# A hybrid attention and delta-rule layer on one core: TensorE's order in the attention stage from fixed to ranked, and its loads moved

## The chip, the core and the metric

The kernel runs on one core of a Trainium2 chip. A core has five engines with queues of their own: TensorE (PE, matrix products, with weight loads shown as PEld), VectorE (DVE), ScalarE (ACT), GpSimd (POOL) and SyncE (SP, which here only issues DMAs). They wait for each other by semaphores. The metric is the device time of one execution in microseconds; smaller is better. Times below are the median of three runs, and the profile is that of one more execution.

## The reference

One layer of a streaming encoder, 1024 frames of 1024 features, float32:

```
u = RMSNorm(h)
p = u @ W_in            # attention q, k, v | delta q, k, v | gate | decay | beta
A = attention(q, k, v)  # 8 heads of 64; each chunk of 64 frames sees itself and 8 chunks before;
                        # q and k normalised per head; bias by clipped distance; softmax
B = gated delta rule    # 4 heads of 128: short causal convolution + SiLU, L2-normalised q, k,
                        # S <- S * decay + k^T (v - k S), output q S, gated RMSNorm per head
h = h + concat[RMSNorm(A), B] @ W_out
h = h + relu(RMSNorm(h) @ W1)^2 @ W2        # 4096 hidden features
```

The output is the (1, 1024, 1024) result.

## The kernel before, in words

A float32 product is made of three products of split operands (`split`: a rounded high part by ScalarE, the low part by VectorE or GpSimd), so a product of large matrices is three matmuls for each step (`mm3`).

The program has four stages. First the input projections for delta k, q, v, the gate, attention k and q and most of attention v, with the preparation of the recurrence beside them. Then the stage that the change touches, `attention`, in which attention, the recurrence, the last two value projections and the beginning of the output projection share TensorE. Then the rest of the output projection, and then the feed-forward layer, `ffn`, whose two halves `ff1` and `ff2` use Strassen-like products of blocks (`product`, q1 to q7 and p1 to p7).

Attention works in 32 units: two groups `g` of four heads, eight tiles `t` of 128 frames, two pairs of heads `pp`. For a unit `score` makes the scores against the newest keys (`t_sb`) and the older ones (`t_sa`), VectorE adds the bias and finds the row limit (L936, L947), ScalarE takes the exponential (L955, L959); `flip` transposes the result on TensorE (`t_tpb`, `t_tpa`) and copies it out by whichever of the two engines is free (`t_tb`, `t_ta`); `multiply` makes the product with the values for both units of a tile (`t_o`), `finish` turns and scales it (`t_on`), `turn` transposes the normalised tile for the output projection (`t_tpo`, `mixa`). The recurrence (`delta_all`) has eight chunks of 128 frames with the steps M (`delta_merge`, `m_tp`, `m_p`), S (`delta_state`, `c_tpv`, `c_pk`, `c_pv`, `c_pq`, `c_pS`), O (`delta_out`, `c_Ltd`, `c_tpq`, `c_mt`, `c_po`) and F (`delta_fin`, `c_tpo`, `mixd`).

All of these share eight PSUM banks: three for scores and projections (`ps_a`), two for transpositions of attention (`ps_t`), one for its output (`ps_o`), two for the recurrence (`ps_d`). Pages of SBUF come from pools by tag; a tile gets a page when an earlier one with the tag is released. Queries of a tile take a page of the tag "x", of which there are two (`start`, L884); biases, keys and values take pages of "u", "dk", "wl" and others as the projections release them.

The order of work is written by a planner: the loop from L1083 keeps a simulated clock (`Clock`) with costs for TensorE, the other engines and the banks, and at each point issues the step that can run soonest, with ties by a rank. START (5000 ns) holds back the first score. The block around it,

```
    with tc.manual_schedule(engines={mybir.EngineType.PE}):
        rest = attention(after[NV - 1], delta_all(ab, kT, W), values, lambda: out_proj(result))
```

keeps TensorE's instructions in exactly the order in which the planner wrote them. On every other engine, and on TensorE outside this block, the scheduler of the language decides at compile time: it goes through the program with its own model of time and issues on each engine, among the instructions whose operands it holds ready, the one that stands first in the code (`tc.high_priority()` moves one ahead; `tc.issue_after(x)` keeps one behind x on its engine). The order that comes out is fixed in the program; on the chip each engine follows its own queue and waits where an operand is late.

The loads of the stage are issued by SyncE. Biases and values first get a small copy on GpSimd from the sixth value projection's result (`after`), so that they don't load earlier. `load_rest` (L869) names the older biases, the remaining values and keys, before tile (0, 2) is scored; the biases of the second group follow at tile (0, 6).

In `ff2`, for each of four blocks of the hidden features, the seven products have operands that VectorE prepares (`prep5`, `prep3`, `prep6`, `prep7`, `prep4`) and that are then split. `early` is the last split of the second product (p5); the first subtraction of `prep3` and of `prep7` is kept behind it on VectorE.

Of the kernel before, what the change touches and what calls it, by code (L numbers as in the profile page):

```python
# [11 lines left out]
ALU = mybir.AluOpType  # L12
# [6 lines left out]
NT = SEQ // P  # L19
# [21 lines left out]
DELTA = 71e3  # L41
LATENCY, MARGIN = 250, 400
LEAD = 0.1
START = 5000
NV = 6


# [52 lines left out]
def hymba_kernel(  # L100
# [20 lines left out]
    nc = tc.nc  # L121
# [708 lines left out]
    def attention(after, delta, values, outputs):  # L830
# [16 lines left out]
        def load_old(g):  # L847
            for i in range(4):
                b = bias_page("u", f"biaso{g}{i}")
                nc.sync.dma_start(out=b[:, 0:384], in_=bias_win[4 * g + i, :, 0:384])  # L850
                nc.gpsimd.memset(b[64:128, 0:64], NEG)
                old[g].append(b)
# [13 lines left out]
                nc.sync.dma_start(out=tl, in_=v_dr[t])  # L866
                vt.append(tl)

        def load_rest():  # L869
            load_old(0)  # L870
            load_values((2, 3))
            load_keys(0, 1)
            load_values(range(4, NT))
            load_keys(1, 0)
            load_keys(1, 1)

        keys, old, new, vt = [[[], []], [[], []]], [[], []], [[], []], []
        load_keys(0, 0)
        load_new(0)
        load_values((0, 1))  # L880

        tiles, outs = {}, {}

        def start(g, t):  # L884
            n = f"t{g}{t}"
            T = dict(n=n, k0=max(0, t - 4))
            T["kb"] = max(0, t - 1)
            if (g, t) == (1, 1):
                T["q"] = [page("on", f"{n}_q{m}", F32R) for m in range(2)]
                for r0 in (0, 64):  # L890
                    for m in range(2):
                        nc.sync.dma_start(out=T["q"][m].bitcast(F32)[r0:r0 + 64], in_=q_dr[t, :, m, g, :])
            else:
                q = page("x", n + "_q", F32R, w=DM)
                qf = q.bitcast(F32)
                for r0 in (0, 64):
                    nc.sync.dma_start(out=qf[r0:r0 + 64].rearrange("p (m c) -> p m c", m=2), in_=q_dr[t, :, :, g, :])
                T["q"] = [part(q, m) for m in range(2)]
            T["sums"] = small("t", n + "_sum", 8)
            T["nm"] = small("t", n + "_nm", 8)  # L900
            T["s"], T["p"], T["done"] = {}, {}, {}
            tiles[g, t] = T

        def product(g, T, i, bk, off, ka, kb):
# [157 lines left out]
        total, spent, deltas, begun, multiplied = sum(size), 0, 0, 0, 0  # L1062
        ready, later, live = [], [], {}
        banks = clock.banks
        groups = delta
        fed = next(groups)

# [15 lines left out]
        while True:  # L1083
# [20 lines left out]
                todo.append((at(flipping[1]), 3, "flip"))  # L1104
            if begun < len(units) and begun - multiplied < 5 and (begun - flipped < 3):
                a = banks["a"]
                todo.append((max(a[0], a[1] - 500, a[2] - 900, START if not begun else 0), 4, "score"))
            if values_left:
                todo.append((banks["a"][0], 7, "values"))
            elif flipped == len(units) and not live.keys() - {"F"} and not any(p[1] is finish and p[2][1] < NT - 1 for p in later):  # L1110
# [10 lines left out]
            if k in live:  # L1121
                gen = live[k][0]
                before = clock.now
                want = next(gen, None)
                deltas += clock.now - before
                if want is None:
                    del live[k]
                else:
                    live[k] = gen, want
            elif k == "multiply":  # L1130
                for n in units[multiplied:multiplied + 2]:
                    multiply(*n)
                    pe(218 * size[multiplied])
                pe(300)
                spent += 2 * size[multiplied]
                t = give("o", on("s", 366, clock.now + LATENCY, ahead=True))
                later.append((t, finish, units[multiplied][0:2]))
                multiplied += 2
            elif k == "later":
                _, step, args = later.pop(0)  # L1140
                step(*args)
                if step is finish:
                    t = give("t", on("v", 420, pe(220), ahead=True))
                    if args[0]:
                        t = on("v", 853, on("g", 3200, on("s", 780, t)))
                        later.append((t + MARGIN, turn, args[1:]))
                        later.sort(key=lambda p: p[0])
                else:
                    give("t", on("v", 682, pe(440), ahead=True))
            elif k == "flip":  # L1150
                want = next(flipping[0], None)
                flipping = want and (flipping[0], want)
                if want is None:
                    flipped += 1
            elif k == "score":
                g, t, pp = units[begun]
                if pp == 0:
                    start(g, t)
                    if (g, t) == (0, 2):
                        load_rest()  # L1160
                    if (g, t) == (0, 6):
                        load_new(1)
                        load_old(1)
                score(g, t, pp)
                begun += 1
            elif k == "values":
                if next(values, None) is None:
                    values_left = False
                else:
                    give("a", on("s", 690, pe(5500)))  # L1170
            else:
                next(outputs_gen)
                pe(690)
                fill += 1
# [231 lines left out]
    def ff2(psw, pools):  # L1406
# [7 lines left out]

        y = {i: [wide(t, 0), wide(t, 1)] for i, t in y.items()}
        y[7] = [page2("y7", f"y7_{i}") for i in range(2)]
        side, splits = [0], []

        def load_h(t, j, hf, m):
            nc.sync.dma_start(out=two(t), in_=h_dr[j, hf, :, 2 * m:2 * m + 2, :])  # L1420
# [1 line left out]
        def product(name, prep, by_rows=False):  # L1422
# [11 lines left out]
            for i in range(2):  # L1434
                ab = []
                for o, src in zip("ab", prep(i)):
                    hi = page2("h" + t, f"{name}{o}{i}_h", F32R)
                    lo = page2("l" + t, f"{name}{o}{i}_l", F32R)
                    splits.append(split(src, hi, lo, nc.scalar, nc.vector)[1])
                    ab.append((hi, lo))  # L1440
                ops.append(ab)
                if not by_rows:
                    for k in range(2):
                        for q in range(4):
                            step(i, k, q)
# [13 lines left out]
        for kb in range(nb):  # L1459
# [50 lines left out]
                return s1[i], b11[i]  # L1510

            def prep3(i):
                with tc.issue_after(early):
                    tt(s1[i], s1[i], a11[i], ALU.subtract)
                tt(a12[i], a12[i], s1[i], ALU.subtract)
                return a12[i], b22[i]

# [2 lines left out]
                return s1[i], b11[i]  # L1520

            def prep7(i):
                with tc.issue_after(early):
                    tt(a21[i], a11[i], a21[i], ALU.subtract)
                tt(b12[i], b22[i], b12[i], ALU.subtract)
                return a21[i], b12[i]

# [3 lines left out]

            accumulate(1, product(f"p1{kb}", lambda i: (a11[i], b11[i])))
            accumulate(5, product(f"p5{kb}", prep5))
            early = splits[-1]
            accumulate(2, product(f"p2{kb}", lambda i: (a12[i], b21[i])))
            if last:
                merge(nc.gpsimd, 2, 1)
# [49 lines left out]
    kT = []  # L1587
# [16 lines left out]
                 att_proj(u, AK, "k"), att_proj(u, AQ, "q"), first_steps(values, NV)), 1.0),  # L1604
        (chained(delta_prep(kT, ab), (1000 for _ in delta_low(0, W, "pp"))), 0.35))
    clock.reset()
    with tc.manual_schedule(engines={mybir.EngineType.PE}):
        rest = attention(after[NV - 1], delta_all(ab, kT, W), values, lambda: out_proj(result))
    for _ in rest or ():
        pass  # L1610
    mixer.close()
# [50 lines left out]
```

## Time and profile before

| what | value |
|---|---|
| median of 3 runs | 1301.49 us (1301.42 to 1302.32) |
| the profiled execution, its time | 1301.99 us |
| its span, first to last instruction | 1300.1 us |
| TensorE busy | 96% of the span |
| VectorE, ScalarE, GpSimd busy | 72%, 42%, 22% |
| mean granted TensorE clock | 0.984 |
| bytes moved by DMA | 158.53 MB, 122 GB/s in the mean |

In the rows of the profile a line such as "371.69 1.19 PE L916 MATMUL t_sb<-ks,t_q ... x4 [6.97 <-DMA t_q<-q_dr]" reads: from 371.69 us for 1.19 us, TensorE, line 916, four matmuls that write `t_sb` from `ks` and `t_q`; before them the engine stood idle for 6.97 us, until a DMA into `t_q` had landed. SPq is the queue in which SyncE issues DMAs. The granted clock (PEclk) is a share of TensorE's full speed.

### The profile page before, as it was taken

The numbers are of one execution on the slowest core, as the hardware profiler recorded it, in microseconds if no ns is written. First come the engines' busy times: TensorE is split into PE (matmuls) and PEld (weight loads), VectorE is DVE, ScalarE is ACT, GpSimd is POOL, SyncE is SP. The second block draws the span as 40 slices with busy tenths as digits, with TensorE's granted clock in tenths as the row PEclk, the third lists the DMA queues.
The fourth block names the chain that finished last, engine by engine and source line by source line (L and its number), as shares of the span: only waits on it lengthen the run. The fifth ranks groups of instructions, "written<-read, shape, count | busy, mean of one in ns | idle before, by whom it ended". The sixth has DMA issues, their size and how long they took to land.

```text
span 1300.1 us, 18013 instructions
## 1 busy us (share of the span) xinstructions
PE 1252.7 (96%) x6686; PEld 1043.8 (80%) x6686; DVE 931.8 (72%) x1389; ACT 546.5 (42%) x898; POOL 289.9 (22%) x487
## 2 busy tenths in 40 slices
PE   9999999999979999879999999999999899999998
PEld 7778878788868988757878788888888688888886
DVE  7899978655036577662529876776668888897998
ACT  7233232232246556463436445444445343333331
POOL 4425451454013344543220000000000000000034
PEclk9999999999979999899999999999999899999999
DMA  6214354566564542123351433332259423413002
GB/s 221 68 47 143 95 150 128 100 169 171 166 210 103 160 105 76 32 85 130 109 169 46 151 118 125 101 114 93 97 194 352 166 97 126 134 61 125 9 33 97
DMA packets 135399, 158.53 MB, mean 122 GB/s; under 512 B 31760, under 2 KB 79376, under 8 KB 134800
## 3 DMA queue, kind: packets, MB, share of 16 engines
q1 hardware_dynamic: 117216, 135.11, 33.9%
q10 hardware_dynamic: 18096, 22.29, 5.0%
q8 instruction: 52, 0.85, 0.3%
q14 instruction: 35, 0.29, 0.1%
HBM read 109.91 MB, written 47.45 MB: 121 GB/s over the span
## 4 chain that ended last, share of the span: by engine, by line
PE 47%; DVE 8%; DMA 3%; ACT 2%; issue 2%; POOL 1%; POOLq 1%; SPq 0%; DVEq 0%; ACTq 0%
PE q L1334 19%; PE p L1430 19%; PE op L223 6%; DMA b<-f_dr 1%; DMA y<-h_dr 1%; PE t_o L1015 1%; DVE h L1276 1%; POOLq L1657 1%; DVE y L1502 0%; DMA h_dr<-h 0%; DVE q_0a_l L205 0%; DMA a<-in_w_ff_dram 0%; PE t_sa L916 0%; DVE y L1498 0%; ACT t_pb L955 0%
## 5 line engine op out<-in xcount | busy, mean ns | idle before, releaser
L1502 POOL TENSOR_TENSOR y<-y,y 128x1024 f32<-128x1024 f32 x6 | 19.3, 3240 | 596.5 <-DVE y L1498 577.7
L1498 DVE TENSOR_TENSOR y<-y,p 128x1024 f32<-128x1024 f32 x46 | 55.3, 1218 | 9.3 <-PE p L1430 8.4
L936 DVE CUSTOM_DVE_ANT_0 t_pb<-t_sb,biasn 128x256 f32<-128x256 f32 (+1 forms) x64 | 23.4, 404 | 41.8 <-PE t_sb L916 41.7
L223 PE MATMUL op<-mh,wo_h 128*128 128x512 f32 x128 | 50.8, 397 | 2.5 <-ACT mh L204 1.1
L223 PE MATMUL op<-ml,wo_h 128*128 128x512 f32 x128 | 50.8, 396 | 0.9 <-DVE ml L205 0.9
L223 PE MATMUL op<-mh,wo_l 128*128 128x512 f32 x128 | 49.3, 394 | 0.5 <-DVE wo_l L205 0.5
L955 ACT ACTIVATE t_pb<-t_pb,t_nm 128x256 f32<-128x256 f32 (+1 forms) x64 | 31.3, 489 | 37.8 <-DVE t_nm L947 34.4
L1221 POOL TENSOR_TENSOR op_q<-op_q 128x512 f32<-128x512 f32 x14 | 20.9, 1496 | 51.4 <-ACT op_q L1220 51.3
L916 PE MATMUL t_sb<-ks,t_q 128*128 128x256 f32 (+1 forms) x144 | 25.6, 310 | 7.0 <-DMA t_q<-q_dr 7.0
L992 PE MATMUL t_tpa<-ident,t_pa 128*128 128x128 f32 x120 | 21.7, 288 | 10.8 <-ACT t_tb L982 6.1
L1214 DVE TENSOR_TENSOR h<-op,op_x 128x512 f32<-128x512 f32 x16 | 11.0, 689 | 28.3 <-PE op L223 28.2
L223 PEld LDWEIGHTS op<-mh,wo_h 128*128 128x128 f32 x128 | 24.2, 189 | 8.7 <-ACT mh L204 1.6
L223 PEld LDWEIGHTS op<-mh,wo_l 128*128 128x128 f32 x128 | 24.3, 190 | 6.6 <-DVE wo_l L205 1.4
L223 PEld LDWEIGHTS op<-ml,wo_h 128*128 128x128 f32 x128 | 24.3, 190 | 6.1 <-DVE ml L205 1.2
L959 ACT ACTIVATE t_pa<-t_pa,t_nm 128x384 f32<-128x384 f32 (+2 forms) x48 | 26.3, 548 | 0.0
L223 PE MATMUL g_ps<-uh,wg_h 128*128 128x512 f32 x64 | 25.3, 396 | 1.0 <-ACT wg_h L204 1.0
L916 PEld LDWEIGHTS t_sb<-ks,t_q 128*128 128x128 f32 x144 | 20.4, 206 | 7.3 <-issue 7.1
L223 PE MATMUL g_ps<-uh,wg_l 128*128 128x512 f32 x64 | 25.2, 393 | 0.4 <-POOL wg_l L205 0.4
L223 PE MATMUL dq_ps<-uh,wdq_h 128*128 128x512 f32 x64 | 25.5, 398 | 0.0
L223 PE MATMUL aq_ps<-waq_h,uh 128*128 128x512 f32 x64 | 25.5, 401 | 0.0
L947 DVE CUSTOM_DVE_ANT_0 t_pa<-t_sa,biaso,t_nm 128x384 f32<-128x384 f32 (+2 forms) x48 | 24.9, 545 | 0.8 <-PE t_o L1015 0.6
L223 PE MATMUL dv_ps<-uh,wdv_l 128*128 128x512 f32 x64 | 25.4, 397 | 0.0
(1109 smaller groups left out, 4333.3 us busy)
## 6 DMA issues: line engine op xcount, KB each, us to landing
wa<-in_w_ff_dram SPq DMA_DIRECT2D x32, 512.0 KB
a<-in_w_ff_dram SPq DMA_DIRECT2D x32, 512.0 KB
b<-f_dr SPq DMA_DIRECT2D x32, 512.0 KB
f_dr<-yy ACTq DMA_DIRECT2D x16, 512.0 KB
t_q<-q_dr SPq DMA_DIRECT2D x30, 256.0 KB
f_dr<-zz ACTq DMA_DIRECT2D x13, 512.0 KB
ks<-k_dr SPq DMA_DIRECT2D x16, 256.0 KB
wo_r<-in_w_out_dram SPq DMA_DIRECT2D x16, 256.0 KB
```

The lines of the kernel that those rows point to most:

```text
L223: nc.tensor.matmul(ps, a, b, start=(first and i == 0), stop=(last and i == n - 1))
L916: nc.tensor.matmul(o, q[m][:, i * P:(i + 1) * P], k[:, c], start=(m == 0), stop=(m == 1))
L936: nc.vector.tensor_tensor_reduce(sb[:, c], bk[:, c], new[g][pp][:, c], -1.0, 3.0e38, ALU.add, ALU.min, nm[:, 4 + i:5 + i])
L947: nc.vector.tensor_tensor_reduce(sa[e][:, 0:wa], bk[:, 0:wa], old[g][i][:, 384 - wa:384], -1.0, nm[:, 4 + i:5 + i], ALU.add, ALU.min, nm[: ...
L955: nc.scalar.activation(sb[:, c], sb[:, c], AF.Exp, bias=m, scale=-1.0, accum_out=T["sums"][:, 4 + i:5 + i])
L959: nc.scalar.activation(sa[e][:, 0:wa], sa[e][:, 0:wa], AF.Exp, bias=m, scale=-1.0, accum_out=T["sums"][:, i:i + 1])
L992: nc.tensor.transpose(tp[:, js], sa[e][:, js], ident)
L1221: nc.gpsimd.tensor_tensor(acc, acc, sq, ALU.add)
L1334: nc.tensor.matmul(part(ps, q), l[:, s], r, start=(k + m == 0), stop=(k == 3 and m == 2))
L1430: nc.tensor.matmul(part(ps[q], 0) if by_rows else part(ps[q // 2], q % 2), l[:, s], part(r, k), start=(i + k + m == 0), stop=(i + k + m == 4))
L1498: nc.vector.tensor_tensor(y[i][m], y[i][m], ps[m], op)
L1502: eng.tensor_tensor(y[i][m], y[i][m], y[z][m], ALU.add)
```

## The change

- The block that fixes TensorE's order is dropped: the planner's order is now only the order in the code, and the scheduler picks among the instructions that are ready on TensorE too.
- `start`, which loads a tile's queries, is called for the first two tiles ahead of the loop and then two tiles ahead, behind the last score of a tile. A tile's first score is planned for 6000 ns behind that call at the earliest, which takes the place of START.
- `load_rest` is cut into parts that follow the scores of tiles (0, 1), (0, 2), (0, 3) and (0, 5).
- In `ff2` the two orders behind `early` are dropped.

```
-START = 5000
...
-        def load_rest():
-            load_old(0)
-            load_values((2, 3))
-            load_keys(0, 1)
-            load_values(range(4, NT))
-            load_keys(1, 0)
-            load_keys(1, 1)
+        def load_rest(t):
+
+            if t == 2:
+                load_old(0)
+                load_values((2, 3))
+            if t == 3:
+                load_keys(0, 1)
+                load_values((4, 5))
+            if t == 4:
+                load_values((6, 7))
+                load_keys(1, 0)
+            if t == 6:
+                load_keys(1, 1)
+                load_new(1)
+                load_old(1)
...
         load_values((0, 1))
+        load_rest(1)
...
+            T["at"] = clock.now + 6000
             tiles[g, t] = T
...
         banks = clock.banks
+        start(0, 0)
+        start(0, 1)
...
-                todo.append((max(a[0], a[1] - 500, a[2] - 900, START if not begun else 0), 4, "score"))
+                todo.append((max(a[0], a[1] - 500, a[2] - 900, tiles[units[begun][0:2]]["at"]), 4, "score"))
...
                 g, t, pp = units[begun]
-                if pp == 0:
-                    start(g, t)
-                    if (g, t) == (0, 2):
-                        load_rest()
-                    if (g, t) == (0, 6):
-                        load_new(1)
-                        load_old(1)
                 score(g, t, pp)
                 begun += 1
+                if pp and begun + 2 < len(units):
+                    start(*units[begun + 2][0:2])
+                if pp and not g:
+                    load_rest(t + 1)
...
             def prep3(i):
-                with tc.issue_after(early):
-                    tt(s1[i], s1[i], a11[i], ALU.subtract)
+                tt(s1[i], s1[i], a11[i], ALU.subtract)
...
             def prep7(i):
-                with tc.issue_after(early):
-                    tt(a21[i], a11[i], a21[i], ALU.subtract)
+                tt(a21[i], a11[i], a21[i], ALU.subtract)
...
-            early = splits[-1]
...
-    with tc.manual_schedule(engines={mybir.EngineType.PE}):
-        rest = attention(after[NV - 1], delta_all(ab, kT, W), values, lambda: out_proj(result))
+    rest = attention(after[NV - 1], delta_all(ab, kT, W), values, lambda: out_proj(result))
```

More of the change, by code (lines that the diff above doesn't have):

```diff
@@ L1416, in ff2 @@
         y[7] = [page2("y7", f"y7_{i}") for i in range(2)]
-        side, splits = [0], []
+        side = [0]
         def load_h(t, j, hf, m):
@@ L1438, in product @@
                     lo = page2("l" + t, f"{name}{o}{i}_l", F32R)
-                    splits.append(split(src, hi, lo, nc.scalar, nc.vector)[1])
+                    split(src, hi, lo, nc.scalar, nc.vector)
                     ab.append((hi, lo))
```

## The prediction

> **What bounds the kernel now.** I read the profile in this order: the page's busy rows, the table of stretches through the attention stage, the waits of TensorE, the order of TensorE's and SyncE's instructions around the longest waits, and last the one other place that the change touches.
>
> ```profile
> span 1300.1 us, 18013 instructions
> PE 1252.7 (96%) x6686; PEld 1043.8 (80%) x6686; DVE 931.8 (72%) x1389; ACT 546.5 (42%) x898; POOL 289.9 (22%) x487
> ```
>
> TensorE is busy for 96% of the span, so the kernel is TensorE-bound as a whole, and only two things can move its time: TensorE's 47.4 us of idle (1300.1 - 1252.7) and the stretches in which its granted clock is lower. No matmul is added or removed. Both losses gather in the stage where attention and the recurrence alternate (about 355 to 582 us). The stretches were cut where the clock or the idle time changes:
>
> ```profile
> core 0: us, PE busy (x) PEld busy (x) DVE busy (x) ACT busy (x) POOL busy (x), PEclk, DMA share, GB/s
> ...
> 364.70:371.70 7.00, 0.03 (x2) 0.05 (x1) 0.65 (x3) 1.59 (x8) 0.00 (x0) 0.68 1.06 331
> 371.70:384.50 12.80, 12.80 (x78) 11.60 (x78) 5.43 (x28) 6.36 (x24) 1.10 (x3) 0.51 0.50 137
> 384.50:418.80 34.30, 32.61 (x336) 29.40 (x333) 23.59 (x76) 21.15 (x65) 15.33 (x33) 0.99 0.40 90
> 418.80:424.60 5.80, 5.80 (x44) 5.74 (x43) 0.56 (x1) 3.40 (x9) 1.06 (x7) 0.50 0.43 101
> 424.60:480.00 55.40, 53.69 (x595) 49.72 (x594) 34.80 (x113) 29.07 (x86) 23.29 (x57) 0.99 0.49 139
> 480.00:531.70 51.70, 46.15 (x430) 41.58 (x428) 36.99 (x117) 33.65 (x107) 24.15 (x68) 1.00 0.29 79
> 531.70:534.60 2.90, 0.01 (x1) 0.00 (x0) 2.90 (x8) 1.20 (x3) 1.26 (x1) 0.98 0.00 0
> 534.60:541.40 6.80, 6.16 (x43) 6.04 (x45) 4.88 (x17) 4.19 (x16) 2.41 (x8) 0.51 0.00 0
> 541.40:577.00 35.60, 28.01 (x263) 24.20 (x259) 21.97 (x49) 20.96 (x51) 16.13 (x41) 1.00 0.20 60
> 577.00:581.90 4.90, 3.32 (x11) 2.62 (x12) 4.58 (x6) 2.90 (x6) 3.03 (x2) 0.69 0.33 107
> ```
>
> Behind the stretch stands its width, then TensorE's busy time; the number ahead of the DMA share is the clock. Width minus busy gives the idle time: 6.97 us up to 371.7; 1.69 + 1.71 + 5.55 = 8.95 us from 384.5 to 531.7; 2.89 + 0.64 + 7.59 + 1.58 = 12.70 us from 531.7 to 581.9. What the low clock costs comes from TensorE's own order around the first gap:
>
> ```profile
> 364.00 0.71 PE L976 MATMUL t_tpb<-ident,t_pb 128*128 128x128 f32 x2
> 371.69 1.19 PE L916 MATMUL t_sb<-ks,t_q 128*128 128x256 f32 x4 [6.97 <-DMA t_q<-q_dr]
> ...
> 373.56 1.12 PE L1015 MATMUL t_o<-t_tb,vt 128*64 128x128 f32 x8
> ...
> 377.40 1.20 PE L916 MATMUL t_sb<-ks,t_q 128*128 128x256 f32 x4
> 378.40 0.95 PE L916 MATMUL t_sa<-ks,t_q 128*128 128x128 f32 x4
> 379.28 1.11 PE L684 MATMUL m_p<-m_sa 64*64 64x64 f32 x8
> ...
> 381.09 1.20 PE L916 MATMUL t_sb<-ks,t_q 128*128 128x256 f32 x4
> ...
> 388.46 0.72 PE L916 MATMUL t_sb<-ks,t_q 128*128 128x256 f32 x4
> 389.02 0.63 PE L916 MATMUL t_sa<-ks,t_q 128*128 128x256 f32 x4
> ```
>
> The same four score matmuls take 1.00 us from start to start at 377.40 and 0.56 us at 388.46, a ratio of 1.79, so 1 - 1/1.79 = 0.44 of the busy time at a clock of 0.5 is loss: 12.80 x 0.44 = 5.6 us, 5.80 x 0.44 = 2.6, 6.16 x 0.44 = 2.7, and in 577.0 to 581.9 (0.69, so about 0.6 of it slow) 3.32 x 0.6 x 0.44 = 0.9. The stage thus loses 12.6 us at its first gap, 8.95 + 2.6 = 11.5 in its middle and 12.70 + 3.6 = 16.3 in its last 50 us, 40 us together. That is all the change can win there.
>
> **The change part by part.** *TensorE's order is freed (L1607).* Before, the matmuls of the stage stand on TensorE exactly as the planner wrote them; an operand that is late stops everything behind it. Afterwards the planned order only ranks the matmuls that are ready by the scheduler's model of time. No instruction is added.
>
> First gap. The wait is for the queries of the third tile, (0, 2). Behind it stood matmuls that don't read them: those from 373.56 to 377.40 (3.84 us from start to start) and from 379.28 to 381.09 (1.81), 5.65 us at the low clock, or 5.65 / 1.79 = 3.2 us at full clock. Freed, they can go into the 6.97 us, and I count 3.2. The rest of the gap is then about 3.8 us, in pieces, so the low clock behind it may or may not come. The bounds of that are 0 and 5.6 us, and I take the middle, 2.8, because the trace has it both ways: after 3.15 us of idle (below) the clock stayed at 1.00, while from 418.8 it was 0.50 though no idle time stands in that stretch. Term: 6.0 us, bounds 0 and 12.6.
>
> [...]
>
> Middle. The idle time of 8.95 us is spread over 147 us. A group of four transposes or score matmuls takes about half a microsecond (0.56 above), so it fits. But the stretches are 89 to 97% busy, and what fills one wait needs its own evacuation by VectorE or ScalarE. I take a quarter, 2.2 us, and nothing of the 2.6 at low clock, which stands beside 32x32 products that stay. Bounds: a loss of 5 (four waits for a bank at the price of the first rival) and a gain of 8.95.
>
> End. The two longest waits of the last part, with what stood behind the second:
>
> ```profile
> 535.24 0.90 PE L992 MATMUL t_tpa<-ident,t_pa 128*128 128x128 f32 x3 [3.53 <-DVE t_ta L997]
> ...
> 542.21 0.66 PE L521 MATMUL c_tpv<-ident,c_jv 128*128 128x128 f32 x4
> 542.71 0.60 PE L521 MATMUL c_tpq<-ident,c_jq 128*128 128x128 f32 x4
> 543.14 1.04 PE L521 MATMUL t_tpo<-ident,t_on 128*128 128x128 f32 x8
> ...
> 556.45 0.55 PE L992 MATMUL t_tpa<-ident,t_pa 128*128 128x128 f32 x3 [3.15 <-ACT t_tb L982]
> 556.83 1.06 PE L517 MATMUL c_po<-c_vn,c_att 128*128 128x128 f32 x8
> 557.65 0.72 PE L916 MATMUL t_sb<-ks,t_q 128*128 128x256 f32 x4
> 558.20 1.07 PE L916 MATMUL t_sa<-ks,t_q 128*128 128x128 f32 x8
> 559.20 0.88 PE L1015 MATMUL t_o<-t_ta,vt 128*64 128x128 f32 x12
> ...
> 574.24 0.47 PE L223 MATMUL op<-mh,wo_h 128*128 128x512 f32 x1
> ```
>
> Both waits are a transposition that wants one of the two transpose banks. Behind the second, `c_po` and the scores of the last tile (556.83 to 559.20, 2.4 us) need no transpose bank; they can run in the 3.15 us. Behind the first, `c_tpv` and `c_tpq` (542.21 to 543.14, 0.9 us) can, and with them in, the idle time is 2.6 us, shorter than the one that kept its clock, so I count its 2.7 us of low clock as saved. Term: 6.0 us. Bounds: 0, if VectorE and ScalarE set the end by themselves (VectorE is busy for all 2.90 us of the first wait), and 16.3.
>
> *Queries two tiles ahead, loads spread, START gone.* I cost them at nothing. No DMA is added; each load keeps its transfer and its small copy on GpSimd. What sets the start of a query load is the slot it writes: two pages hold queries, so those of (0, 2) wait for the scores of (0, 0), at 362 us, whoever asks first. SyncE's queue shows it:
>
> ```profile
> 352.14 2.60 SPq L850 DMA_DIRECT2D biaso<-in_rel_bias_dram  x4
> ...
> 356.88 2.06 SPq L859 DMA_DIRECT2D ks<-k_dr  x4
> ...
> 362.46 1.06 SPq L859 DMA_DIRECT2D ks<-k_dr  x2
> ...
> 364.53 2.51 SPq L897 DMA_DIRECT2D t_q<-q_dr  x4
> ```
>
> In the code the query load stood ahead of the rest, and yet the rest was issued first, as soon as its pages were free. Moving it later in the code only lowers its rank on SyncE and GpSimd; nothing new holds it back. Bounds: 0, and the whole wait with its clock, 12.6 us, if the spread does keep the DMA engines (share 1.06 here) free for the queries; if it makes keys or values late instead, one wait like that one, -7.0. The new 6000 ns before a tile's scores only moves ranks. Between them I take 0, since the issue order is the nearest row.
>
> *The two orders dropped in the second feed-forward product (L1513, L1523).* Four subtractions may now go ahead of the last split of the second product:
>
> ```profile
> 992.95 1.22 DVE L205 TENSOR_TENSOR p50b_l<-b,p50b_h 128x1024 fp32r<-128x1024 f32 x1
> 994.09 1.22 DVE L1514 TENSOR_TENSOR s<-s,a 128x1024 f32<-128x1024 f32 x1
> ```
>
> ```profile
> 1019.00:1027.00 8.00, 6.58 (x17) 5.26 (x18) 8.00 (x8) 0.00 (x0) 0.00 (x0) 0.57 0.88 284
> ```
>
> They stood right behind it, on a VectorE that was busy, so I take 0. Ahead of it they would delay it by up to 4 x 1.14 = 4.6 us (loss); if the order further on gets better, TensorE's idle time and low clock at 1019 to 1027 could go, 1.4 + 6.58 x 0.86 x 0.44 = 3.9 us (gain).
>
> Sum: the profiled execution took 1301.99 us (span 1300.1 and 1.9 around it); 1302.0 - 6.0 - 2.2 - 6.0 = 1287.8. The median of the runs is 0.5 lower than that execution, so 1287.3.
>
> **The rivals.** *Slower: banks taken out of order.* Two transpose banks, two for the recurrence, one for the attention output serve every chain. Freed, a transposition of lower rank that is ready takes a bank as it falls free, and the planned one waits one evacuation longer.
>
> ```profile
> PE t_tpa L992 <- ACT t_tb L982: 6.1, 5, 3.1
> ```
>
> One such wait is 6.1 / 5 = 1.2 us. The 24 units with an old part take a transpose bank three times each; from 12 uncovered waits on (14.2 / 1.2) the gain is gone, and at 24 it is 1302 + 24 x 1.2 - 14 = 1316. For it: the bank waits of the end already are the longest. Against it: from 384.5 to 480 TensorE is 96% busy and such a wait is covered. Chance 0.22.
>
> *It doesn't do what it says:* the third tile's scores are ranked into the gap again because the model thinks their queries arrive early, and the end is held by VectorE and ScalarE. Then only the middle gains: 1301.5 - 2.2 = 1299.3. For it: the issue order above, and VectorE full at 531.7. Chance 0.18. [...]
>
> *Larger:* the loads are in fact spread, the first loss goes whole (12.6), and the end gives 11: 1301.5 - 12.6 - 2.2 - 11 = 1275.7. Against it: the same issue order. Chance 0.12.
>
> **How the numbers follow.** The forecast (1280 to 1297, chance 0.48) is the likeliest: 1287.3. The range reaches from 1275, the larger gain, to 1305, which takes in the unchanged case and the start of the slower one; beyond lie about 0.04 below and 0.15 above. A change under 0.2%, 2.6 us, can't be told from none here. Faster: 0.48 + 0.12 + 0.08 of the unchanged case = 0.68; same: 0.10; slower: 0.22.
>
> **What would show it.** Right: TensorE's order has merge, `t_o` and `t_tpb` matmuls ahead of the scores of (0, 2); its idle time from the first score to the first 20 us of the output projection falls by about 10 us; the wait of 3.15 us is filled by `c_po` and scores; the first output-projection matmul (574 us before) comes about 12 to 14 us earlier, and everything from there on keeps its length. The loads' part is wrong if SyncE issues `ks` and `vt` well after 364 us. The prediction fails if the bank waits (`t_tpa`, `t_tpb`, `t_on`) grow, if the wait for `t_q` stands as before, or if the stretch from 975 to 1027 us changes by more than 4 us.

## The result and the profile after

The changed kernel takes 1282.16 us (median of four runs, 1278.61 to 1285.73) against 1301.90 us of the kernel before beside it: a ratio of 0.9844, 95% interval 0.9813 to 0.9875. Measured again with the experiments it took 1277.62 us against 1302.78 us, 0.9823 (0.9801 to 0.9845). The profiled execution of the changed kernel is the longest of its four, 1285.73 us.

The first rows of its page; line numbers have moved by up to 9 (scores L925, flips L985 and L1001, `p` L1438, `op` L222):

```profile
span 1283.8 us, 18012 instructions
PE 1258.0 (98%) x6686; PEld 1039.6 (81%) x6686; DVE 924.8 (72%) x1388; ACT 548.3 (43%) x899; POOL 289.9 (23%) x487
```

TensorE's idle time fell from 47.4 to 25.8 us (1283.8 - 1258.0). The attention stage in stretches of the same widths, counted from about the end of the last value projection (361.4 us before, 368.7 us after); behind each stretch its width, then TensorE's busy time, and the clock ahead of the DMA share. Before:

```profile
361.40:384.40 23.00, 15.95 (x101) 13.99 (x102) 8.08 (x42) 10.06 (x37) 2.20 (x6) 0.63 0.75 231
384.40:421.40 37.00, 35.31 (x363) 32.04 (x359) 23.59 (x76) 23.08 (x70) 15.33 (x33) 0.96 0.43 98
421.40:481.40 60.00, 58.29 (x623) 54.32 (x622) 36.65 (x119) 32.05 (x96) 24.35 (x63) 0.97 0.46 131
481.40:521.40 40.00, 36.15 (x349) 32.63 (x349) 29.00 (x97) 27.75 (x91) 18.70 (x52) 1.00 0.32 87
521.40:561.40 40.00, 30.66 (x271) 28.19 (x269) 26.64 (x71) 20.16 (x55) 16.35 (x45) 0.91 0.10 25
561.40:586.40 25.00, 19.44 (x130) 14.85 (x127) 18.30 (x27) 14.32 (x33) 14.18 (x32) 0.93 0.36 111
```

After:

```profile
368.70:391.70 23.00, 23.00 (x210) 19.93 (x208) 15.09 (x63) 15.76 (x52) 10.28 (x19) 1.00 0.77 217
391.70:428.70 37.00, 34.97 (x343) 30.55 (x344) 19.07 (x63) 18.73 (x58) 10.67 (x30) 0.86 0.51 132
428.70:488.70 60.00, 59.29 (x555) 50.88 (x553) 36.58 (x123) 35.84 (x109) 22.10 (x56) 1.00 0.46 130
488.70:528.70 40.00, 39.53 (x348) 34.45 (x349) 30.19 (x96) 25.27 (x79) 18.56 (x52) 1.00 0.28 77
528.70:568.70 40.00, 35.66 (x319) 29.85 (x319) 31.12 (x82) 28.48 (x73) 22.55 (x64) 1.00 0.13 37
568.70:593.70 25.00, 24.29 (x121) 19.89 (x118) 11.87 (x17) 8.61 (x15) 13.25 (x20) 1.00 0.44 137
```

Over these 225 us TensorE is busy for 216.7 instead of 195.8 us. The first gap is gone whole, with its low clock (0.63 to 1.00); the last 65 us have 5.1 us of idle time instead of 14.9, and no low clock. Only the second stretch is worse: its clock is 0.86. TensorE's order shows what fills the gap:

```profile
368.71 0.38 PE L985 MATMUL t_tpb<-ident,t_pb 128*128 128x128 f32 x2
368.85 1.15 PE L925 MATMUL t_sb<-ks,t_q 128*128 128x128 f32 x8
...
370.53 0.66 PE L520 MATMUL c_tpv<-ident,c_jv 128*128 128x128 f32 x4
371.12 0.44 PE L1024 MATMUL t_o<-t_tb,vt 128*64 128x128 f32 x4
...
372.50 1.06 PE L516 MATMUL c_pv<-c_jv,m_yb 128*128 128x128 f32 x8
...
375.17 1.16 PE L516 MATMUL c_pS<-c_vn,c_kt 128*128 128x128 f32 x8
...
379.19 0.72 PE L925 MATMUL t_sb<-ks,t_q 128*128 128x256 f32 x4
```

The scores of tile (0, 2) stand at 379.19, and ahead of them stand flips, products with the values and nearly the whole first chunk of the recurrence (`c_tpv`, `c_pv`, `c_pS`), more than the prediction had counted there. TensorE's waits:

```profile
PE l_p L640 <- issue: 2.0, 1, 2.0
PE p L1438 <- DVE p50b_l L204: 1.8, 1, 1.8
PE t_tpb L985 <- ACT t_on L1053: 1.6, 2, 1.3
PE t_tpa L1001 <- ACT t_tb L991: 1.6, 3, 0.7
```

The 7 us for `t_q` are gone. The waits of `t_tpa` for a bank are down from 6.1 and 3.5 us to 1.6. Also gone is a wait outside the stage, in the second feed-forward product, 4.7 us for `p30b_l`.

Marks of the two profiled executions, from the first and last rows of the named matmuls, place the 16.3 us of span:

| stretch | before | after | difference |
|---|---|---|---|
| start to first `aq_ps` | 263.8 | 265.9 | +2.1 |
| first `aq_ps` to last `av_ps` | 97.4 | 102.6 | +5.2 |
| last `av_ps` to first `q` (attention, output projection) | 310.5 | 291.9 | -18.6 |
| first `q` to first `p` | 305.4 | 306.4 | +1.0 |
| first `p` to the end (`ff2`) | 323.0 | 317.0 | -6.0 |

Part of the 5.2 us are 20 merge matmuls (`m_tp`, `m_p`) that moved ahead of the last value projection. In a second profiled execution of the same program (span 1275.8) this stretch takes 100.3 us and the stage 286.8: the stage differs by 5 us between two executions of one program, which is taken up at the end. The first row's 2.1 us are no effect of the change: in the executions profiled for the experiments this stretch takes 263.7 to 265.8 us, 265.6 in one whose edit lies in `ff2` alone.

### The profile page after: what moved, and what is told of

Same layout as the page of the kernel before. It is cut to its first block, busy times and chain, and to the rows that moved or that the text cites. A ratio compares the mean times of both kernels' runs of the same rounds, so it can differ in the third digit from the quotient of the medians.

```text
span 1283.8 us, 18012 instructions
## 1 busy us (share of the span) xinstructions
PE 1258.0 (98%) x6686; PEld 1039.6 (81%) x6686; DVE 924.8 (72%) x1388; ACT 548.3 (43%) x899; POOL 289.9 (23%) x487
## 4 chain that ended last, share of the span: by engine, by line
PE 72%; DVE 8%; DMA 3%; POOL 2%; issue 2%; ACT 1%; POOLq 1%; SPq 0%; ACTq 0%; DVEq 0%
PE p L1438 20%; PE q L1342 20%; PE op L222 5%; PE av_ps L222 3%; PE aq_ps L222 3%; PE g_ps L222 3%; PE t_o L1024 3%; PE ak_ps L222 2%; PE t_sb L925 1%; PE t_sa L925 1%; PE t_tpb L985 1%; PE t_tpa L1001 1%; DMA wa<-in_w_ff_dram 1%; PE c_pv L516 1%; PE c_mt L516 1%
## 5 line engine op out<-in xcount | busy, mean ns | idle before, releaser
L222 PE MATMUL op<-mh,wo_h 128*128 128x512 f32 x128 | 50.1, 393 | 0.9 <-ACT wo_h L203 0.8
L222 PE MATMUL op<-ml,wo_h 128*128 128x512 f32 x128 | 49.9, 391 | 0.0
L222 PE MATMUL op<-mh,wo_l 128*128 128x512 f32 x128 | 48.6, 393 | 0.7 <-POOL wo_l L204 0.7
L1024 PE MATMUL t_o<-t_ta,vt 128*64 128x128 f32 x240 | 29.3, 292 | 0.3 <-DVE t_ta L1006 0.3
L222 PEld LDWEIGHTS op<-mh,wo_h 128*128 128x128 f32 x128 | 24.0, 188 | 6.6 <-ACT wo_h L203 1.2
L222 PEld LDWEIGHTS op<-mh,wo_l 128*128 128x128 f32 x128 | 24.0, 188 | 6.1 <-POOL wo_l L204 1.0
L222 PEld LDWEIGHTS op<-ml,wo_h 128*128 128x128 f32 x128 | 24.0, 188 | 5.0
L222 PE MATMUL aq_ps<-waq_h,uh 128*128 128x512 f32 x64 | 26.2, 412 | 1.1 <-ACT waq_h L203 1.1
L222 PE MATMUL g_ps<-uh,wg_h 128*128 128x512 f32 x64 | 25.3, 396 | 1.4 <-ACT wg_h L203 1.4
L222 PE MATMUL aq_ps<-waq_l,uh 128*128 128x512 f32 x64 | 25.6, 406 | 0.0
L222 PE MATMUL g_ps<-uh,wg_l 128*128 128x512 f32 x64 | 25.2, 393 | 0.4 <-POOL wg_l L204 0.4
L222 PE MATMUL dq_ps<-uh,wdq_h 128*128 128x512 f32 x64 | 25.5, 398 | 0.0
L222 PE MATMUL dv_ps<-uh,wdv_l 128*128 128x512 f32 x64 | 25.4, 397 | 0.0
L222 PE MATMUL aq_ps<-waq_h,ul 128*128 128x512 f32 x64 | 25.4, 400 | 0.0
```

The costliest lines, as they stand in the source:

```text
L222: nc.tensor.matmul(ps, a, b, start=(first and i == 0), stop=(last and i == n - 1))
L1024: nc.tensor.matmul(po[64 * e:64 * e + 64, pp * P:(pp + 1) * P], vt[k0 + j][:, 64 * h:64 * h + 64], (ta[e] if j < na else tb)[:, c:c + P], ...
```

## The experiments

The theory (A in the expectations): the freed order gains by filling each wait where it stands, the moved loads are worth nothing beside it, and the two dropped orders gain by themselves. The rivals are named with each. Ratios are against the kernel before, run beside on the same chip, in three groups: one to four, five to eight, nine to twelve. Gains in us are differences of medians; the ratios put them up to some 2 us lower.

**Each part alone.** First: the kernel before with TensorE's order freed and nothing else.

```
-    with tc.manual_schedule(engines={mybir.EngineType.PE}):
-        rest = attention(after[NV - 1], ...)
+    rest = attention(after[NV - 1], ...)
```

> The kernel before with one edit: TensorE's order in the attention stage is freed; the loads and the two orders in the second feed-forward product stay as before. Theory A (the freed order carries the gain of the attention stage, the loads little): the wait of 6.97 us for the third tile's queries shrinks to under 3 us, the stretch from the last value projection to the first feed-forward matmul shrinks by 16 to 19 us (310.1 before, 291.5 after the whole change), and the wait of 4.7 us in the second feed-forward product stays; the time is 1288, between 1284 and 1292. Theory B (the moved loads remove the first gap): the wait for the queries stays at 5 us or more, and the time is about 1296.

Measured 1283.47 us against 1302.99, 0.9861 (0.9840 to 0.9882): the freed order alone gives 19.5 us (18.1 by the ratio), more than I had expected.

Second: the kernel before with only the two orders behind `early` dropped.

```
-                with tc.issue_after(early):
-                    tt(s1[i], s1[i], a11[i], ALU.subtract)
+                tt(s1[i], s1[i], a11[i], ALU.subtract)
...
-                with tc.issue_after(early):
-                    tt(a21[i], a11[i], a21[i], ALU.subtract)
+                tt(a21[i], a11[i], a21[i], ALU.subtract)
```

> The kernel before with one edit: the two orders behind the last split of the second product are dropped; attention is as before. Theory A (the dropped orders by themselves made the second feed-forward product 5.9 us shorter): its length from the first matmul to the end goes from 323.2 to about 317.3 us, the wait of 4.7 us for p30b_l goes, and the time is about 1296. Rival (that product is shorter after the change only because it is reached in another state of the queues): length 323 us, time 1302 as before.

Measured 1296.53 us, 0.9966 (0.9950 to 0.9981): 6.5 us by the medians, 4.4 by the ratio, for a part that the prediction put at nothing. In the profiled execution `ff2` itself takes 318.7 us instead of 323.0.

Third: the changed kernel with those two orders put back, so the freed order with the moved loads.

```
...
+                with tc.issue_after(early):
+                    tt(s1[i], s1[i], a11[i], ALU.subtract)
...
+                with tc.issue_after(early):
+                    tt(a21[i], a11[i], a21[i], ALU.subtract)
```

> The changed kernel with the two orders in the second feed-forward product put back, so the freed order and the moved loads together. Theory A: as the run with the freed order alone, within 2 us, about 1288, with the wait for p30b_l back. Theory B (loads matter beside it): 5 us or more faster than the freed order alone.

Measured 1283.02 us, 0.9854 (0.9832 to 0.9876): the loads add nothing to the freed order that can be told (0.9861 without).

Fourth: the moved loads alone, in TensorE's fixed order.

```
 # the third kernel, with
+    with tc.manual_schedule(engines={mybir.EngineType.PE}):
+        rest = attention(after[NV - 1], ...)
```

> The kernel before with the moved loads and the 6000 ns before a tile's scores, TensorE's order still fixed and the two orders in the second feed-forward product kept. Theory A: the queries of the third tile still wait for their page (362 us) and for the DMA engines; TensorE waits 5 us or more for them, the low clock behind it stays, and the time is 1302, within 3 us. Theory B: the wait and the low clock go, about 1289.

Measured 1300.00 us, 0.9982 (0.9967 to 0.9996): 3 us (2.3 by the ratio). TensorE's order at its wait for the queries:

```profile
365.03 0.44 PE L1024 MATMUL t_o<-t_tb,vt 128*64 128x128 f32 x4
...
367.17 0.66 PE L985 MATMUL t_tpb<-ident,t_pb 128*128 128x128 f32 x4
...
371.84 1.23 PE L925 MATMUL t_sb<-ks,t_q 128*128 128x256 f32 x4 [3.80 <-DMA t_q<-q_dr]
```

The wait is down from 6.97 to 3.80 us, but not because the queries come earlier. SyncE issues them at 364.60 us (364.53 in the kernel before), and the scores that need them start at 371.84 (371.69 before). What differs is the plan: products with the values, merge matmuls and flips, which stood behind these scores in the kernel before (from 373.56 us), now stand ahead of them. That fits the 6000 ns, before which the planner places no first score of a tile. No run has the 6000 ns without the moved loads, so the two are not separated. But the queries' arrival, which the loads could have moved, is unchanged, so "costed at nothing" was right for the loads, and it was the new plan that filled 3.2 us.

**Which of the two orders in `ff2`, and why.** Fifth, for reference, the changed kernel again.

> The changed kernel once more, on the chip of the next three runs, as their measure. Theory A (the freed order and the two dropped orders gain apart from each other, 19.5 and about 6 us): less than the 1283.0 of the run with the freed order and the loads but with the two orders put back, 1278 to 1281; after the first q product everything as in the first look at it (the second feed-forward product 317 us). Rival B (the two gains overlap): 1282 to 1284, no better than that run.

1277.62 us, 0.9823 (0.9801 to 0.9845): below the third kernel's 0.9854, as expected if the gains add. Sixth and seventh: it with one order put back.

```
 sixth (with `early` defined again, as in the seventh):
...
+                with tc.issue_after(early):
+                    tt(a21[i], a11[i], a21[i], ALU.subtract)      # prep7
 seventh:
+                with tc.issue_after(early):
+                    tt(s1[i], s1[i], a11[i], ALU.subtract)        # prep3
```

> Of the two orders in the second feed-forward product the one of prep7 is put back, that of prep3 stays dropped. Theory A (what pays is that the splits of p3 now stand ahead of those of p6 on VectorE): this kernel's queue has p60a_l and p60b_l ahead of p30a_l and p30b_l again, so the wait of 4.7 us for p30b_l and the low clock behind it come back: 5 to 6 us slower than the changed kernel. Rival B (what pays is that the first subtraction of prep3 runs ahead of the split p50b_l): that is the case here, so it is as fast as the changed kernel, within 1 us.

> The other half: the order of prep3 is put back, that of prep7 stays dropped. Theory A: p30a_l and p30b_l stay ahead of p60a_l and p60b_l, no wait for p30b_l; and as one subtraction less (1.1 us) stands ahead of the split p50b_l, the changed kernel's wait of 1.8 us for it shrinks to about 0.7: as fast as the changed kernel or up to 1.1 us faster. Rival B: the gain is gone, 5 to 6 us slower than the changed kernel.

The sixth took 1282.67 us, 0.9856 (0.9838 to 0.9874), the seventh 1278.05 us, 0.9817 (0.9795 to 0.9838). Prep7's order costs the 5 us, prep3's nothing. But the wait that comes back in the sixth is not the expected one; its row in TensorE's order:

```profile
987.82 0.73 PE L1438 MATMUL p<-p20b_h,p20a_h 128*128 128x512 f32 x2 [3.94 <-ACT p20b_h L203]
```

It is for a split made by ScalarE. So I read ScalarE's order, first of the kernel before:

```profile
990.49 1.05 ACT L204 CAST p50b_h<-b 128x1024 fp32r<-128x1024 f32 x1
998.92 0.37 ACTq L1343 DMA_DIRECT2D f_dr<-yy  x1
999.39 1.01 ACT L1496 COPY y<-p 128x1024 f32<-128x1024 f32 x1 [7.85 <-DMA y<-h_dr]
```

and of the changed kernel:

```profile
981.30 1.05 ACT L203 CAST p20a_h<-a 128x1024 fp32r<-128x1024 f32 x1
982.26 1.00 ACT L1504 COPY y<-p 128x1024 f32<-128x1024 f32 x1
983.16 1.04 ACT L203 CAST p50b_h<-b 128x1024 fp32r<-128x1024 f32 x1
984.10 1.01 ACT L1504 COPY y<-p 128x1024 f32<-128x1024 f32 x1
988.41 0.37 ACTq L1351 DMA_DIRECT2D f_dr<-yy  x1
```

ScalarE issues the last store of the first product's result (`f_dr<-yy`), and the issue waits for an earlier transfer. The semaphores in the trace say for which: the store raises the same semaphore as the first load of `y<-h_dr`, which SyncE issued at 988.48 us, and ScalarE holds the store until that load has landed, at 998.85 us. It needs nothing from that load, and its own data had been ready since 990.76 us. Before, the store stands ahead of the copies of p1 and the splits of p2, so ScalarE does nothing for 7.85 us; after, two copies and two splits stand ahead of it, and 3.71 us of idle time are left. The store itself goes off at the same point, 15.05 us behind the first split of p5 before (998.92 - 983.87) and 14.86 us after (988.41 - 973.55). The orders on VectorE thus had an effect on ScalarE: they changed the compile-time order there.

The ninth run tests this: the third kernel, both orders in place, with the last four of these stores moved to GpSimd.

```
-                nc.scalar.dma_start(out=f_dr[...], in_=two(t))
+                (nc.gpsimd if sb == 7 else nc.scalar).dma_start(out=f_dr[...], in_=two(t))
```

> TensorE's order freed, the loads moved and both orders of the second feed-forward product in place, as in the third run (1283.0 us, 0.9854), with one edit: the last four stores of the first product's result (f_dr) are issued by GpSimd and not by ScalarE. Theory A, new: the two orders matter through ScalarE's queue. With them the issue of the store of yy stands ahead of the copies of p1 and of the first split of p2, and ScalarE stands still for 7.5 us until an earlier transfer has landed; TensorE sees it later as the wait of 4.7 us for p30b_l. Then this kernel is 5 us faster than the third run, about 0.982 of before, and the wait for p30b_l is gone although p60a_l and p60b_l still stand ahead of p30a_l on VectorE. Rival B: VectorE's order of p30 and p60 decides; then nothing changes, 0.985, wait of 4.7 us as before.

Measured 1276.28 us, 0.9805 (0.9787 to 0.9822). The gain is there with both orders in place and with p60's splits still ahead of p30's in VectorE's program. Its ScalarE order and its row among TensorE's waits:

```profile
974.98 1.05 ACT L203 CAST p20a_h<-a 128x1024 fp32r<-128x1024 f32 x1
975.93 1.91 ACT L1504 COPY y<-p 128x1024 f32<-128x1024 f32 x2
977.74 1.06 ACT L203 CAST p20b_h<-b 128x1024 fp32r<-128x1024 f32 x1
```

```profile
PE p L1438 <- DVE p30b_l L204: 1.6, 1, 1.6
```

ScalarE goes straight on. On GpSimd the last of the stores is issued as soon as VectorE has finished its data (974.73 us). In the profiled executions `ff2` takes 317.1 us here and 322.0 in the third run. The wait for `p30b_l` shrinks from 4.7 to 1.6 us; I had expected it to be gone. The store in ScalarE's queue is thus shown as the cause of most of the gain in `ff2`. The order of p30 and p60, my theory for the sixth and seventh runs, explains at most the 1.6 us that are left. What the wait cost beyond itself stands in the stretch around it, 21.5 us of the kernel before and then of the changed kernel:

```profile
1010.40:1031.90 21.50, 16.80 (x63) 13.38 (x62) 19.13 (x17) 9.03 (x10) 0.00 (x0) 0.84 0.47 153
```

```profile
1000.00:1021.50 21.50, 21.50 (x97) 17.80 (x96) 21.50 (x20) 9.92 (x10) 0.00 (x0) 1.00 0.61 201
```

4.7 us of idle time and a clock of 0.84 before, neither after.

**The loads once more.** Eighth: the kernel before with the freed order and without prep7's order, the loads as they were. It differs from the seventh only in the loads, the calls of `start` and the 6000 ns.

```
-    with tc.manual_schedule(engines={mybir.EngineType.PE}):
...
-                with tc.issue_after(early):
-                    tt(a21[i], a11[i], a21[i], ALU.subtract)
+                tt(a21[i], a11[i], a21[i], ALU.subtract)
```

> The kernel before with TensorE's order freed and prep7's order dropped; the loads, START and the calls of start stay as before. It differs from the run with prep3's order put back only in the loads and the 6000 ns. Theory A (beside a freed order the moved loads are worth nothing, since other matmuls fill the wait for the queries): the same time within 1.5 us. Rival B (the loads keep the 3 us that they gained alone): 3 us slower.

Measured 1277.57 us, 0.9821 (0.9798 to 0.9844), the seventh 0.9817: beside the freed order the loads and the 6000 ns together are worth nothing that can be told.

**Where in the stage the freed order gains.** Tenth: the kernel before, freed up to the first score of tile (0, 3). Eleventh: fixed up to the first score of tile (1, 4), freed behind it.

```
 tenth: at begun == 6, eleventh: the other way round, at begun == 24
...
+                if begun == 6:
+                    fixed.enter_context(tc.manual_schedule(engines={mybir.EngineType.PE}))
                 score(g, t, pp)
```

> The kernel before with TensorE's order freed only until tile (0, 3) is scored, and fixed again from there to the end of the stage. Theory A (each wait is filled in its place and the time stays won): the first gap of 12.6 us goes in whole, 1289 to 1291; the waits of the end (t_tpa 6.1 and 3.5 us) stand as before. Rival B (what is won at the head is given back later, since VectorE and ScalarE set the end): less than 4 us, 1298 to 1302, with more idle time after 400 us.

Measured 1300.24 us, 0.9987 (0.9978 to 0.9997): 2.4 us, in the rival's range. But not by the rival's mechanism. Two rows of its TensorE order:

```profile
374.71 1.19 PE L916 MATMUL t_sb<-ks,t_q 128*128 128x256 f32 x4 [4.66 <-DMA t_q<-q_dr]
...
386.42 0.72 PE L916 MATMUL t_sb<-ks,t_q 128*128 128x256 f32 x4
```

The wait was filled by 2.3 us only (4.66 for 6.97) and the scores behind it still run at the low clock (1.19 us, where those at 386.42 take 0.72; the clock is 0.61 from 370 to 380 us). What was won stays: the scores of 386.42 stand at 388.46 in the kernel before, 2.0 us later; the first output matmul stands at 574.2 us there and at 572.3 here, and the span is 2.2 us longer there. Nothing is given back. The cut was too near: the recurrence's first chunk, which fills the gap in the changed kernel, comes behind (0, 3) in the plan.

> The complement: TensorE's order fixed as before until tile (1, 4) is scored, and freed from there. Theory A: the wait for the queries stands (7 us) and the rest of the 19.5 us that the freed order brought, some 7, comes from here: 1294 to 1297, the waits for t_tpa down to about 2 us in sum; the middle brings next to nothing. Rival B: the end is held by VectorE and ScalarE, or most of it comes from the middle: 1299 to 1302.

Measured 1290.04 us, 0.9908 (0.9891 to 0.9924): 12.6 us, above A's 7. Up to about 486 us its order is that of the kernel before. From there to the first output matmul, first the kernel before, then this one:

```profile
485.60:574.20 88.60, 72.38 (x670) 65.12 (x668) 59.79 (x167) 53.02 (x151) 41.77 (x110) 0.96 0.20 54
```

```profile
485.90:559.50 73.60, 69.86 (x611) 60.93 (x609) 54.65 (x159) 47.34 (x140) 37.41 (x99) 0.98 0.22 61
```

16.2 us of idle time before, 3.7 after (88.60 - 72.38, 73.60 - 69.86), at a VectorE that is busy for 74% instead of 67%: VectorE and ScalarE did not hold the end. In the second stretch 59 matmuls fewer are done, which now follow among those of the output projection; counted to the first `q`, the stage is 12.1 us shorter (298.4 for 310.5). The two parts make 15.0 of the 19.5 us. The other 4.5 lie in the steps between, or in what these would have put into the first gap; no run separates that.

**What the low clock costs.** Twelfth: the kernel before with 60 idle products ahead of the scores of (0, 2).

```
             bk = bank(ps_a, f"{n}_sb{pp}")
+            if (g, t, pp) == (0, 2, 0):
+                for i in range(60):
+                    nc.tensor.matmul(bk[:, 0:P], ident, ident, start=True, stop=True)
```

> The kernel before, order fixed, with 60 more matmuls of the identity with itself (128x128, into the bank that the scores of tile (0, 2) then overwrite) ahead of those scores, so that TensorE is busy while it waits for the queries; no useful work is moved. Theory A (the gap costs twice: 7.0 us idle and 5.6 us of low clock behind it): the clock stays at 1.00 from 371 to 385 us and the time falls by 5 to 6 us, to 1296 or 1297. Rival B (the low clock there comes for another reason, as from 418.8 us, where no idle time stands): no change, or up to 1 us slower.

Measured 1303.76 us, 1.0014 (1.0003 to 1.0025): slower by 1.2 us (1.8 by the ratio), close to Rival B's number, but not for its reason. The 60 products took longer than I had thought. In its TensorE order and its stretches:

```profile
364.79 13.56 PE L929 MATMUL t_sb<-ident 128*128 128x128 f32 x120
...
390.41 0.70 PE L916 MATMUL t_sb<-ks,t_q 128*128 128x256 f32 x4
```

```profile
364.80:378.10 13.30, 13.30 (x121) 13.30 (x121) 0.79 (x5) 1.74 (x8) 0.00 (x0) 1.00 0.74 228
378.10:391.00 12.90, 11.84 (x118) 10.17 (x117) 6.64 (x31) 9.26 (x33) 2.67 (x6) 1.00 0.37 101
```

They ran for 13.3 us and pushed the scores of (0, 2) from 371.69 to 378.11, 6.4 us later. The clock stayed at 1.00, and at 390.41 the kernel is only 1.95 us behind the one before (388.46): the full clock won back 4.5 us. Between these marks TensorE's busy time falls from 16.53 to 11.23 us, by 5.3, which is near the 5.6 that the prediction had worked out; 0.8 us of it comes back as short waits. Rival B, a low clock for another reason, falls: with TensorE kept busy (13.30 of 13.30 us) the clock was 1.00 there and over the 12.90 us behind. The 2.0 us of delay are still there at the first output matmul (576.2 against 574.2).

## Why the prediction was right

The result, 1282.2 us, lies in the forecast's own range (1280 to 1297) and below its 1287.3. The repeated measurement, 1277.6 us, lies just below that range and inside the outer one (1275 to 1305). Step by step:

- *TensorE-bound, two losses.* Right as to where the time goes, but the sum has a term missing. In the stage, from the last `av_ps` to the first `q`, TensorE's idle time falls from 31.5 to 10.1 us, 21.4 less, and the clock rises from 0.95 to 0.98. The busy time should then have fallen by some 7.7 us, an estimate from the prediction's 11.8 us of low-clock loss before (5.6 + 2.6 + 2.7 + 0.9) and the 4.1 us after that the last section works out. It rose by 2.9 us instead (279.0 to 281.9). So the new order costs some 10 us of busy time for the matmuls themselves, which the prediction put at nothing. Why is not shown by any run.
- *First gap, 6.0 us taken of 12.6.* Mis-sized in its parts, near in what is left of them. I counted as filler only what stood within 10 us behind the wait in the fixed order, 3.2 us. Freed, the matmuls of a whole chunk came forward, and the gap went whole, with its low clock. A part is paid for earlier, where merge work now stands ahead of the last value projection. If the medians can be subtracted, the head and the middle together give 6.9 us (19.5 of the first run less 12.6 of the eleventh), where 8.2 were forecast. Of the low clock behind the gap the forecast took half, 2.8 of 5.6 us; all of it went: the 23.00 us from 368.7 have a clock of 1.00, with the transposes `t_tpb`, `c_tpv` and `t_on` among other products.
- *Middle, 2.2 us.* The number is near by luck. I took a quarter of the idle time and nothing of the clock. From 384.4 to 521.4 us idle time was 7.25 us; in the matching stretches after it is 3.21, so 4.0 less. The first of the three stretches has a clock of 0.86 for 0.96, which by estimate costs 3.3 us (0.1 is 0.2 of the time at 0.5: 37 x 0.2 x 0.44), the second 1.00 for 0.97, which gives 1.6 (60 x 0.06 x 0.44): 2.3 us in all.
- *End, 6.0 us, bounds 0 and 16.3.* Mis-sized: 12.6 us by the eleventh run (12.0 by its ratio). I costed the two longest waits alone. But the whole stretch from 486 us to the output projection had 16.2 us of idle time in many pieces, and 12.5 of it went.
- *Loads, 0.* Right beside the freed order (0.9821 without, 0.9817 with), and for the reason given: SyncE still issues keys and values ahead of the queries,

```profile
364.49 2.01 SPq L858 DMA_DIRECT2D ks<-k_dr  x4
366.98 2.40 SPq L865 DMA_DIRECT2D vt<-v_dr  x3
369.43 0.90 SPq L858 DMA_DIRECT2D ks<-k_dr  x2
370.42 0.55 SPq L905 DMA_DIRECT2D t_q<-q_dr  x1
```

  Wrong was that the 6000 ns only move ranks: in the fixed order a rank is the order itself, and the wait falls to 3.8 us.
- *The two orders in `ff2`, 0, bounds a loss of 4.6 and a gain of 3.9.* Wrong outright: 4 to 6.5 us (the second run, and the sixth against the fifth), beyond my bound of 3.9. I looked at VectorE, where the instructions are, and at the stretch in which TensorE waited. The 4.7 us wait for `p30b_l` ended in that stretch, and I did not follow it back to ScalarE's 7.85 us behind a store. My own sign of failure, a change of more than 4 us there, came.
- *Rival: banks out of order, 1316.* Refuted: the waits of `t_tpa` for a bank went from 9.6 to 1.6 us, and those of `t_tpb` for `t_on` stayed (1.5 and 1.6). *Rival: it doesn't do what it says.* Refuted by the first run. *Rival: larger, 1275.7.* Its size for the end (11) was nearer than mine. For the head it took the whole 12.6 us because of spread loads, a reason that did not hold.

The gain was forecast too small, by 5.1 us in the first measurement and by 9.7 in the second. What it lacked is the end and `ff2`. It did not come out further off because the new order also costs time that the prediction had not counted: the merge matmuls ahead of the stage, the longer busy time, and in some executions a low clock behind 408 us. That these nearly cancel in the first measurement is luck. Of the signs, the first output matmul came 14.5 us earlier (559.7 for 574.2), near the 12 to 14 foreseen, but the idle time fell by 21 us, not 10.

## What to carry to other kernels

Where an order written by hand stands on the engine that bounds the kernel, look at what may overtake each wait, and count far: a whole independent chain can come forward, not only the next few instructions. A wait found on one engine is followed back to the engine that made its operand and to what stands in that engine's queue: here a DMA issue with a wait of its own held the compute behind it for 7.85 us, and an order given to VectorE at compile time moved that of ScalarE. A part that "costs nothing" deserves its own run.

## What the runs showed of the hardware that was not expected

The clock. Two executions of the changed kernel, 8.0 us apart in span, differ most at one place, a first group of 32x32 products (`l_p`). In the first execution:

```profile
409.09 1.42 PE L640 MATMUL l_p<-l_w,l_xa 32*32 32x32 f32 x32 [2.03 <-issue]
```

```profile
408.00:420.00 12.00, 10.91 (x101) 9.60 (x102) 3.92 (x16) 4.18 (x12) 0.00 (x0) 0.57 0.45 120
```

In the second execution:

```profile
404.40 1.17 PE L640 MATMUL l_p<-l_w,l_xa 32*32 32x32 f32 x32 [0.40 <-issue]
```

```profile
403.00:415.00 12.00, 11.60 (x163) 10.32 (x163) 6.84 (x24) 7.12 (x23) 2.38 (x8) 1.00 0.46 122
```

With 2.03 us of idle time the clock is 0.57 over the 12 us that follow, about 4 us of loss by estimate (0.57 is 0.86 of the time at 0.5, and 10.91 x 0.86 x 0.44 is 4.1); with 0.40 us it is 1.00. The same wait was 1.32, 1.40, 1.66 and 2.18 us in the third, seventh, ninth and sixth runs, and the clock from 405 to 410 us was 0.69, 0.66, 0.71 and 0.50 there. In these six executions the clock was 0.71 or less with 1.32 us and more, and 1.00 with 0.40 us. But before the change 3.15 us of idle time kept a clock of 1.00 (541.4 to 577.0 us), and the eighth kernel kept 1.00 over idle times of 2.0 and 1.3 us. So the length of the wait alone does not decide it; what else does stays open. The kernel before has such a place too: just ahead of its stretch of 0.50 from 418.8 us, in which the prediction saw no idle time, TensorE had waited 0.72 us ahead of `l_p`. Such waits are also what is late next: with the first gap filled, TensorE next waits 0.4 to 2.5 us, at 390 to 410 us, in every profiled execution with the order freed throughout. They are for later queries, or ahead of `l_p` probably for loads of `l_xa`: the row names no releaser, but SyncE still issues such loads up to 408.3 us in the first execution.
